# A two-block transformer in split fp32: high and low activations in one 512-column matmul

## Chip, core and metric

The kernel runs on one core of a Trainium2 chip. The metric is device time in microseconds from the first to the last instruction of the program, median of the runs; lower is better.

## What is computed

One call runs two transformer blocks over 256 positions of width 2048, all in fp32. The core of the reference:

```
x = x + hybrid_mixer(rms_norm(x), w_in, ...)          # causal pooling + gated delta net
x = x + memory_cross_attention(rms_norm(x), mem_h, w_xq, w_xkv, w_xo)
x = x + conv_glu_ffn(rms_norm(x), w_gate, w_up, ..., w_down)     # width 5632 ("FFN 1")
x = rms_norm(x, final_norm_g)
h = modulate(rms_norm_2(x, pre_norm_mix), shift_m, scale_m)
x = x + gate_m * rms_norm_2(concat(nsa_mixer(h), moba_mixer(h)) @ w_o, ...)
h = modulate(rms_norm_2(x, pre_norm_ffn), shift_f, scale_f)
x = x + gate_f * rms_norm_2(square(relu(h @ w_up)) @ w_down, ...)  # width 8192 ("FFN 2")
```

Nearly all arithmetic is in products of the 256 activations with large weights.

## The kernel before

**Split products.** A product keeps fp32 accuracy by splitting both factors into a high part (rounded to TensorE's fp32r type) and a low part (the rest). Of the four partial products three are computed: high times high, high weight times low activation, low weight times high activation. ACT writes the high weights (`wh`, L216), DVE subtracts to get the low ones (`wl`, L218).

**Units.** Weights come in groups of 512 columns of a weight matrix over all contraction blocks of 128 rows (`kb`). A unit is 1024 columns per partition, 512 KB: two contraction blocks of 512 columns. The class `Group` lists them, and `plan` fixes the order of all 880 for the whole program. `take` (called as each unit is reached) puts the split of the unit two ahead and the load of the unit up to seven ahead into the instruction streams; there are four buffers for loaded units and three for split ones.

**The two linear forms.** `lin_a` keeps activations stationary and streams 512 weight columns (L300 to L302). `lin_b` (L304) keeps 128x128 weight blocks stationary and streams the 256 activations, so that its output is transposed: features on partitions. For each contraction block and each of the four column blocks it issues three 256-column matmuls (L318 high·high, L319 high weight·low activation, L320 low weight·high activation) into the same half of a PSUM bank:

```
mm(ps, wb, h, ...); mm(ps, wb, lo, ...); mm(ps, wb2, h, ...)
```

A group of `lin_b` fills two of four accumulator banks (`acc`). 62 groups go this way: eight of `w_in`, four keys, four queries, 22 of gate and up in FFN 1, eight of the second mixer, 16 of FFN 2's up.

**Evacuation.** What follows a product is a Python generator: each `yield` ends a step, and `pump` (after every unit) lets each running task emit one step. `group_start` lets at most one older evacuation be unfinished: an older one is made to emit all that is left, at once. Engines execute their streams in order, so this fixes where each step stands. `rr_evac` multiplies each accumulator by the row of rms factors (`rr`), `conv_evac` and `gate_evac` go on with a convolution and a silu, `pool_evac` with running sums on POOL and one small matmul per window (L845), `up_evac`, `relu_evac` and `rope_evac` with their functions. `conv_evac` waits for `rr`, which a task `stats` makes from the loaded x at the start of the program (squares on ACT L378, sum on DVE L348, power on POOL L341, then two matmuls, L361). `ada` is a long background task on DVE (L1200).

**Activations.** `act_pair` holds them in four tiles: two with the high parts of 16 contraction blocks, two with the low parts.

Of the kernel before, what the change touches and what calls it, by code (L numbers as in the profile page):

```python
# [15 lines left out]
P = 128  # L16
# [73 lines left out]

class Prog:
# [3 lines left out]
    def __init__(self, ctx, tc, i, o, dbg=None):  # L95
# [16 lines left out]
        self.rr = None  # L112

# [192 lines left out]
    def lin_b(self, g, xh, xl, evac, ready=None):  # L306
        mm = self.nc.tensor.matmul
        accs = self.group_start()
        for _, kb0, nk in g.units:
            self.check_ready(ready, kb0)  # L310
            wh, wl = self.take(g)
            for k in range(nk):
                kb = kb0 + k
                h, lo = xh(kb), xl(kb)
                for b in range(4):
                    ps = accs[b // 2][:, (b % 2) * T:(b % 2 + 1) * T]
                    wb, wb2 = wh[:, k, b * P:(b + 1) * P], wl[:, k, b * P:(b + 1) * P]
                    mm(ps, wb, h, start=kb == 0 and b % 2 == 0, stop=False, skip_group_check=True)  # L318
                    mm(ps, wb, lo, start=False, stop=False, skip_group_check=True)  # L319
                    mm(ps, wb2, h, start=False, stop=kb == g.nkb - 1, skip_group_check=True)  # L320
            self.pump()
        return self.finish_group(evac([a.rearrange("p (b t) -> p b t", b=2) for a in accs]))
# [93 lines left out]
    def act_pair(self, half):  # L416

        a = [self.t(f"A{4 * half + j}", [P, 8, T], F32R) for j in range(4)]

        def part(o):  # L420
            return lambda kb, n=0: a[o + kb // 8][:, kb % 8:kb % 8 + n] if n else a[o + kb // 8][:, kb % 8, :]

        return part(0), part(2)
# [77 lines left out]
    def run(self):  # L501
# [4 lines left out]
        for n, a in (("k0", 2048), ("q0", 1024), ("v0", 3072), ("z0", 4096), ("u0", 0), ("u1", 512), ("k1", 2560),  # L506
                     ("q1", 1536), ("v1", 3584), ("z1", 4608)):
            g_in[n] = G(w_in, [(a, a + 512)])
# [4 lines left out]
        mk, mv = cols(i["w_xkv"], 4), cols(i["w_xkv"], 4, D)  # L513
        mix = [cols(i["w_mix_out"], 4, 0, 1024 * s, 8) for s in range(2)]
        xq = cols(i["w_xq"], 4)
        xo = [cols(i["w_xo"], 4, 0, 1024 * s, 8) for s in range(2)]
        self.gate, self.up = cols(i["w_gate"], 11), cols(i["w_up"], 11)
# [6 lines left out]
        b2["nq"] = cols(w2, 2)  # L524
        b2["nk1"] = G(w2, [(1024, 1536)])
        b2["nk2"] = G(w2, [(1536, 1792), (2048, 2304)])
        b2["nv"] = G(w2, [(1792, 2048), (2304, 2560)])
        b2["mq"], b2["mk"], b2["mv"] = cols(w2, 2, 2584), cols(w2, 2, 3608), cols(w2, 2, 4632)
        b2["wo"] = [cols(i["w_o_2"], 4, 0, 1024 * s, 8) for s in range(2)]
        b2["wo"][1][3:] = [G(i["w_o_2"], [(a, a + 256)], 1024, 8) for a in (1536, 1792)]  # L530
        self.up2 = cols(i["w_up_2"], 16)
# [87 lines left out]
        for name in ("silu_c", "gl16"):  # L619
            self.col(name, KB)  # L620
# [3 lines left out]
        conv0 = [self.lin_b(g_in["k0"], xh, xl, lambda a: self.conv_evac(a, S[0]["k"], "k0", 0),  # L624
                            ready={4 * c: lt[c] for c in range(4)})]
        conv0.append(self.lin_b(g_in["q0"], xh, xl, lambda a: self.conv_evac(a, S[0]["q"], "q0", 0)))
        self.start(self.ba_task(xh, xl))
        conv0.append(self.lin_b(g_in["v0"], xh, xl, lambda a: self.conv_evac(a, S[0]["v"], "v0", 0)))
# [4 lines left out]
        pools = [self.lin_b(g_in["u0"], xh, xl, lambda a: self.pool_evac(a, 0))]  # L633
        pools.append(self.lin_b(g_in["u1"], xh, xl, lambda a: self.pool_evac(a, 1)))
        conv1 = []
        for n, tag in (("k1", "r4"), ("q1", "r5"), ("v1", "r6")):
            S[1][n[0]] = self.t(tag, [P, 4, T])
            conv1.append(self.lin_b(g_in[n], xh, xl, lambda a, n=n: self.conv_evac(a, S[1][n[0]], n, 4)))
# [21 lines left out]
        def key_evac(a, c):  # L660
            yield from self.wait_for(ypt)
            kT[c] = self.t(["r8", "r9", "r7", "r11"][c], [P, 4, T])
            yield from self.rr_evac(a, kT[c], self.rrm)

        for c in range(4):
            self.lin_b(mk[c], mh, ml, lambda a, c=c: key_evac(a, c),
                       ready={4 * q: mt[q] for q in range(4)} if c == 0 else None)
# [36 lines left out]
        for c in range(4):  # L704
            qT.append(self.t(["r5", "r6", "r3", "r10"][c], [P, 4, T]))
            ev = self.lin_b(xq[c], xh, xl, lambda a, c=c: self.rr_evac(a, qT[c], self.rr))
# [30 lines left out]
    def rr_evac(self, accs, dst, row):  # L737
        for h in range(2):
            self.nc.vector.tensor_tensor(dst[:, 2 * h:2 * h + 2], accs[h], row[:, None, :].to_broadcast([P, 2, T]),
                                         op=OP.mult)  # L740
            yield
# [12 lines left out]
    def conv_evac(self, accs, dst, n, h0):  # L754
        nc = self.nc
        yield from self.until(lambda: self.rr is not None)
        st = self.t("A7" if n[0] == "q" else "A6", [P, 4, T])
        for h in range(2):
            nc.vector.tensor_tensor(st[:, 2 * h:2 * h + 2], accs[h], self.rr[:, None, :].to_broadcast([P, 2, T]),
                                    op=OP.mult)  # L760
            yield
        blk0 = {"q": 0, "k": 8, "v": 16}[n[0]] + h0
        cw = self.par("dn_conv_w")
        for b in range(4):
# [7 lines left out]
        nc.scalar.activation(dst, dst, AF.Silu)  # L772
# [42 lines left out]
    def pool_evac(self, accs, c):  # L815
        nc = self.nc
        u = self.t("r7", [P, 4, T])
        if c == 0:
# [5 lines left out]
        yield from self.rr_evac(accs, u, self.rr)  # L824
        buf = self.t("r11", [P, 2, 2, T])
        for j in range(2):
            wi = 2 * c + j
            ub = u[:, 2 * j:2 * j + 2]
            cur = ub
            for lv in range(wi + 1):  # L830
                d = 1 << lv
                nxt = buf[:, lv % 2]
                nc.gpsimd.tensor_tensor(nxt[:, :, d:], cur[:, :, d:], cur[:, :, :T - d], op=OP.add)
                nc.scalar.activation(nxt[:, :, :d], cur[:, :, :d], AF.Copy)
                cur = nxt
            yield
            mx = buf[:, wi % 2]
            nc.vector.tensor_tensor(mx, mx, self.inv[:, wi][:, None, :].to_broadcast([P, 2, T]), op=OP.mult)
            nc.vector.tensor_tensor(mx, mx, ub, op=OP.subtract)
            yield  # L840
            tag, ps = yield from self.get_bank()
            psv = ps.rearrange("p (b t) -> p b t", b=2)
            for hb in range(2):
                for gb in range(2):
                    nc.tensor.matmul(psv[:, hb], self.wpl[:, wi, gb, hb * P:(hb + 1) * P], mx[:, gb],  # L845
                                     start=gb == 0, stop=gb == 1)
            yield
            for hb in range(2):
                kb = 2 * wi + hb
                nc.scalar.activation(self.yp[c][:, 2 * j + hb], psv[:, hb], AF.Copy, scale=self.pcol("pool_scale")(kb))  # L850
            self.give(tag)
# [383 lines left out]
    def gate_evac(self, accs, c):  # L1235
        nc = self.nc
        st = self.t(f"r{c % 2}", [P, 4, T])
        cv = self.t(f"r{2 + c % 2}", [P, 4, T])
        self.cv[c] = cv
        rr = self.rr[:, None, :].to_broadcast([P, 2, T])  # L1240
        for h in range(2):
# [753 lines left out]
```

## Time and profile before

| | |
|---|---|
| median of 3 runs | 2728.45 us (2722.99 to 2728.89) |
| the profiled execution's own time | 2727.51 us |
| its span | 2725.7 us |
| TensorE busy | 2681.1 us, 98% of the span |
| DVE / ACT / POOL busy | 68% / 48% / 9% |
| DMA | 584 MB, 214 GB/s on average |

Matmuls overlap in the pipeline, so the duration of one (283 ns) is not what it costs; the distance from one start to the next is. A timeline shows it directly: the difference of two starts divided by the number of matmuls between them. "Idle before" in the groups says how long an engine stood still, and for whom.

### The profile page before, as it was taken

What the parts mean: (1) busy time and instruction counts of PE and PEld (TensorE: products, weight loads), DVE (VectorE), ACT (ScalarE), POOL (GpSimd) and SP (SyncE); (2) the same over time, 40 slices, a digit from 0 to 9 for tenths busy, and PEclk for the clock granted to TensorE, in tenths of its full rate; (3) what the DMA queues carried; (4) which work ended last, traced back from release to release, by engine and by line L of the source; (5) the groups of instructions that cost most, each with busy time, mean ns of one, the idle gap of its engine ahead of it and who ended that gap; (6) DMA issues with size and microseconds to landing.
All of it is one profiled execution on the core that took longest, in us unless ns stands there. A gap on an engine that the chain in (4) does not pass through costs nothing.

```text
span 2725.7 us, 45971 instructions
## 1 busy us (share of the span) xinstructions
PE 2681.1 (98%) x18466; PEld 2480.4 (91%) x18466; DVE 1854.2 (68%) x2331; ACT 1302.8 (48%) x1924; POOL 255.5 (9%) x229
## 2 busy tenths in 40 slices
PE   8999999999999999999999999999989999999998
PEld 8999998889989999999999888997889988999897
DVE  6665745677687778787778586677675556655555
ACT  6544533554445455354544564444554444444443
POOL 0230211000000021010100001001011000000020
PEclk9999999999999999999999999999999999999999
DMA  8644644688788888888887656544557767766654
GB/s 290 201 126 130 191 121 140 216 295 272 228 270 266 272 259 272 275 265 283 271 270 263 210 164 178 147 146 128 173 181 235 236 218 241 232 190 193 189 186 151
DMA packets 293126, 584.33 MB, mean 214 GB/s; under 512 B 21920, under 2 KB 36384, under 8 KB 292912
## 3 DMA queue, kind: packets, MB, share of 16 engines
q1 hardware_dynamic: 288528, 568.41, 65.6%
q0 software_dynamic: 3664, 11.67, 1.4%
q8 instruction: 145, 2.38, 0.4%
q10 hardware_dynamic: 720, 1.31, 0.1%
q14 instruction: 69, 0.57, 0.1%
HBM read 579.21 MB, written 2.10 MB: 213 GB/s over the span
## 4 chain that ended last, share of the span: by engine, by line
PE 93%; DVE 3%; ACT 2%; issue 1%; POOL 0%; DMA 0%; SPq 0%; DVEq 0%; POOLq 0%; ACTq 0%
PE acc L318 16%; PE acc L319 16%; PE acc L320 16%; PE acc L300 12%; PE acc L301 12%; PE acc L302 12%; DVE wl L218 1%; ACT wh L216 1%; PE m L998 1%; PE m L1051 1%; PE m L1058 1%; PE m L1148 1%; PE m L1117 1%; PE m L1001 0%; PE m L1179 0%
## 5 line engine op out<-in xcount | busy, mean ns | idle before, releaser
L218 DVE TENSOR_TENSOR wl<-w,wh 128x1024 fp32r<-128x1024 f32 x880 | 1097.1, 1249 | 805.2 <-ACT wh L216 802.8
L216 ACT ACTIVATE wh<-w 128x1024 fp32r<-128x1024 f32 x880 | 927.9, 1058 | 1121.4 <-PE acc L319 614.3
L318 PE MATMUL acc<-A,wh 128*128 128x256 f32 x3968 | 1124.1, 283 | 9.3 <-ACT A L406 7.8
L319 PE MATMUL acc<-A,wh 128*128 128x256 f32 x3968 | 1112.6, 280 | 0.7 <-DVE A L1430 0.7
L320 PE MATMUL acc<-A,wl 128*128 128x256 f32 x3968 | 1112.0, 280 | 0.8 <-DVE wl L218 0.8
L318 PEld LDWEIGHTS acc<-A,wh 128*128 128x128 f32 x3968 | 750.6, 189 | 11.4 <-ACT A L406 7.8
L320 PEld LDWEIGHTS acc<-A,wl 128*128 128x128 f32 x3968 | 756.7, 191 | 1.0 <-DVE wl L218 1.0
L319 PEld LDWEIGHTS acc<-A,wh 128*128 128x128 f32 x3968 | 749.2, 189 | 2.6 <-DVE A L1430 1.2
L300 PE MATMUL acc<-wh,A 128*128 128x512 f32 (+1 forms) x1584 | 616.0, 389 | 0.3 <-DVE r L1264 0.3
L301 PE MATMUL acc<-wl,A 128*128 128x512 f32 (+1 forms) x1584 | 608.3, 384 | 1.2 <-DVE wl L218 1.2
L302 PE MATMUL acc<-wh,A 128*128 128x512 f32 (+1 forms) x1584 | 607.8, 384 | 0.0
L301 PEld LDWEIGHTS acc<-wl,A 128*128 128x128 f32 x1584 | 298.1, 188 | 60.5 <-DVE wl L218 4.5
L302 PEld LDWEIGHTS acc<-wh,A 128*128 128x128 f32 x1584 | 297.8, 188 | 59.3
L300 PEld LDWEIGHTS acc<-wh,A 128*128 128x128 f32 x1584 | 298.0, 188 | 57.2 <-issue 0.9
L1200 DVE SCALAR_TENSOR_TENSOR r<-r,c_silu_c,r 128x1024 f32<-128x1024 f32 x128 | 170.1, 1329 | 0.0
L1200 DVE SCALAR_TENSOR_TENSOR s<-s,c_silu_c,s 128x512 f32<-128x512 f32 x128 | 95.8, 748 | 15.7 <-DMA s<-w_ada 14.4
L1886 POOL TENSOR_TENSOR s<-s 128x512 f32<-128x512 f32 x32 | 50.9, 1592 | 581.5 <-ACT s L1885 581.5
L1255 POOL TENSOR_TENSOR r<-r,rr 128x1024 f32<-128x1024 f32 x11 | 27.9, 2536 | 570.3 <-ACT r L1254 527.5
L1730 ACT ACTIVATE s<-s,c_am 128x128 f32<-128x128 f32 (+1 forms) x48 | 21.5, 448 | 92.0 <-DVE c_am L1728 92.0
L1618 POOL TENSOR_TENSOR r<-r,s 128x512 f32<-128x512 f32 x15 | 25.6, 1704 | 263.7 <-DVE s L1615 263.7
L1251 DVE SCALAR_TENSOR_TENSOR r<-r,prm,r 128x254 f32<-128x254 f32 x88 | 42.4, 481 | 1.6
L378 ACT ACTIVATE dd<-X 128x512 bf16<-128x512 f32 (+1 forms) x42 | 25.5, 606 | 21.4 <-DVE X L441 15.6
(375 smaller groups left out, 1611.8 us busy)
## 6 DMA issues: line engine op xcount, KB each, us to landing
w<-w_up SPq DMA_DIRECT2D x216, 512.0 KB, 3.8
w<-w_down SPq DMA_DIRECT2D x216, 512.0 KB, 3.9
w<-w_in SPq DMA_DIRECT2D x152, 512.0 KB, 3.7
r<-w_ada SPq DMA_DIRECT2D x128, 512.0 KB, 5.2
w<-w_gate SPq DMA_DIRECT2D x88, 512.0 KB, 4.3
w<-w_xkv SPq DMA_DIRECT2D x64, 512.0 KB, 3.9
s<-w_ada SPq DMA_DIRECT2D x128, 256.0 KB, 5.1
w<-w_mix_out SPq DMA_DIRECT2D x32, 512.0 KB, 3.7
```

The costliest lines, as they stand in the source:

```text
L216: nc.scalar.activation(hi[:, :m], src[:, :m], AF.Copy)
L218: eng.tensor_tensor(lo[:, :m], src[:, :m], hi[:, :m].bitcast(F32), op=OP.subtract)
L300: mm(ps, h, wh[:, k, :], start=kb == 0, stop=False)
L301: mm(ps, h, wl[:, k, :], start=False, stop=False)
L302: mm(ps, lo, wh[:, k, :], start=False, stop=kb == g.nkb - 1)
L318: mm(ps, wb, h, start=kb == 0 and b % 2 == 0, stop=False, skip_group_check=True)
L319: mm(ps, wb, lo, start=False, stop=False, skip_group_check=True)
L320: mm(ps, wb2, h, start=False, stop=kb == g.nkb - 1, skip_group_check=True)
L1200: nc.vector.scalar_tensor_tensor(acc, tiles.pop(n), self.silu_c[:, kb:kb + 1], acc, op0=OP.mult, op1=OP.add)
L1251: nc.vector.scalar_tensor_tensor(cv[:, b, s:], st[:, b, :T - s], w[k], cv[:, b, s:], op0=OP.mult, op1=OP.add)
L1255: nc.gpsimd.tensor_tensor(cv, cv, self.rr[:, None, :].to_broadcast([P, 4, T]), op=OP.mult)
L1886: nc.gpsimd.tensor_tensor(y, y, y, op=OP.mult)
```

## The change

The high and low activations of one contraction block now lie next to each other, so that one matmul with a high weight block streams both, 512 columns; the low weight block adds its 256 into the second half. One PSUM bank then holds high·high in its first half and the two cross products in the second, and the evacuation adds the halves first (`fold`): ACT copies the second half out, DVE adds the first. A 512-wide group becomes a `Pair` of two 256-wide ones, each of four units of four contraction blocks (same bytes, rows of 1 KB instead of 2 KB), each with its two banks and its own evacuation. The first pairs of six stages (`widen`) run unit by unit side by side in all four banks.

```
+class Pair:
+    def __init__(self, w, a, b=None):
+        self.subs = [Group(w, [(c, c + 256)]) for c in (a, b)]
+        self.units = self.subs[0].units + self.subs[1].units
+    def widen(self):
+        self.units = [u for two in zip(*(g.units for g in self.subs)) for u in two]
...
+    def lin_b(self, pair, xh, xl, evac, ready=None):
+        if pair.wide:
+            while self.evacs:
+                self.need(self.evacs.pop(0))
+            accs = [[self.acc(), self.acc()] for _ in range(2)]
...
+    def unit_b(self, g, n, accs, xh, ready):
...
+            for b in range(2):
+                mm(accs[b], wb, xh.both(kb).rearrange("p j t -> p (j t)"), start=kb == 0, ...)
+                mm(accs[b][:, T:], wb2, xh(kb), start=False, stop=kb == g.nkb - 1, ...)
+    def fold(self, accs, dst):
+        for b in range(2):
+            self.nc.scalar.activation(dst[:, b], accs[b][:, 1], AF.Copy)
+            self.nc.vector.tensor_tensor(dst[:, b], accs[b][:, 0], dst[:, b], op=OP.add)
...
-        a = [self.t(f"A{4 * half + j}", [P, 8, T], F32R) for j in range(4)]
+        a = [self.t(f"A{4 * half + j}", [P, 4, 2, T], F32R) for j in range(4)]
...
+        for p in (g_in["k0"], mk[0], xq[0], self.gate[0], b2["nk1"], self.up2[0]):
+            p.widen()
...
     def rr_evac(self, accs, dst, row):
-        for h in range(2):
-            self.nc.vector.tensor_tensor(dst[:, 2 * h:2 * h + 2], accs[h], row[...], op=OP.mult)
+        self.fold(accs, dst)
+        yield
+        self.nc.vector.tensor_tensor(dst, dst, row[...], op=OP.mult)
...
     def pool_evac(self, accs, j, c):
...
         nc.vector.tensor_tensor(mx, mx, ub, op=OP.subtract)
+        for _ in range(3):
+            yield
         tag, ps = yield from self.get_bank()
```

The other evacuations change alike: fold, a step, then what they did before, on half the columns per task.

**First place: TensorE, from the program's first group (`k0`) to its second (`q0`).** Rows are line, operation, out<-in, shape. Before, the two matmuls that make `rr` (from `dd`) stand inside `q0`, after the first matmuls of its third unit:

```order
L320 MATMUL acc_23_421<-A_5_98,wl_424 128x256
L318 MATMUL acc_24_422<-A_5_98,wh_423 128x256
L319 MATMUL acc_24_422<-A_7_100,wh_423 128x256
L320 MATMUL acc_24_422<-A_5_98,wl_424 128x256
L318 MATMUL acc_24_422<-A_5_98,wh_423 128x256
L319 MATMUL acc_24_422<-A_7_100,wh_423 128x256
L320 MATMUL acc_24_422<-A_5_98,wl_424 128x256
L361 MATMUL m_26_521<-dd_488,cst 128x128 x2
```

Now they stand right ahead of `q0`'s first matmul:

```order
L355 MATMUL acc_14_120<-A_8_101,wl_279 128x256
L353 MATMUL acc_13_119<-A_8_101,wh_278 128x512
L355 MATMUL acc_13_119<-A_8_101,wl_279 128x256
L353 MATMUL acc_14_120<-A_8_101,wh_278 128x512
L355 MATMUL acc_14_120<-A_8_101,wl_279 128x256
L401 MATMUL m_27_374<-dd_371,cst 128x128 x2
L353 MATMUL acc_30_391<-A_5_98,wh_308 128x512
L355 MATMUL acc_30_391<-A_5_98,wl_309 128x256
L353 MATMUL acc_31_392<-A_5_98,wh_308 128x512
L355 MATMUL acc_31_392<-A_5_98,wl_309 128x256
```

Each triple of 256-column matmuls has become a 512-column and a 256-column one, and the `rr` matmuls have moved three units forward.

**The same place on DVE.** Before, the weight splits (`wl`) go on, and the first group's evacuation (L759) begins between the splits of later units:

```order
L218 TENSOR_TENSOR wl_354<-w_8_203,wh_353 128x1024
L218 TENSOR_TENSOR wl_388<-w_9_238,wh_387 128x1024
L218 TENSOR_TENSOR wl_424<-w_10_273,wh_423 128x1024
L348 TENSOR_REDUCE c_mix_r_s<-c_mix_p 128x2
L218 TENSOR_TENSOR wl_459<-w_11_319,wh_458 128x1024
L357 TENSOR_SCALAR dd_488<-cst,c_mix_r 128x128
L218 TENSOR_TENSOR wl_492<-w_12_357,wh_491 128x1024
L759 TENSOR_TENSOR A_29_528<-acc_11_116,rr_524 128x512
L218 TENSOR_TENSOR wl_531<-w_13_391,wh_530 128x1024
L759 TENSOR_TENSOR A_29_528<-acc_12_117,rr_524 128x512
```

Now the fold (L362) and the whole evacuation of the first half of `k0` stand between the splits of units 9 and 10 (`w_9_...` and `w_10_...`):

```order
L234 TENSOR_TENSOR wl_335<-w_9_217,wh_334 128x1024
L362 TENSOR_TENSOR A_25_360<-acc_11_117,A_25_360 128x256
L362 TENSOR_TENSOR A_25_360<-acc_12_118,A_25_360 128x256
L388 TENSOR_REDUCE c_mix_r_s<-c_mix_p 128x2
L397 TENSOR_SCALAR dd_371<-cst,c_mix_r 128x128
L813 TENSOR_TENSOR A_25_360<-A_25_360,rr_377 128x512
L821 SCALAR_TENSOR_TENSOR A_9_112<-A_25_360,prm,A_9_112 128x253
L821 SCALAR_TENSOR_TENSOR A_9_112<-A_25_360,prm,A_9_112 128x254
L821 SCALAR_TENSOR_TENSOR A_9_112<-A_25_360,prm,A_9_112 128x255
L821 SCALAR_TENSOR_TENSOR A_9_112<-A_25_360,prm,A_9_112 128x253
L821 SCALAR_TENSOR_TENSOR A_9_112<-A_25_360,prm,A_9_112 128x254
L821 SCALAR_TENSOR_TENSOR A_9_112<-A_25_360,prm,A_9_112 128x255
L234 TENSOR_TENSOR wl_394<-w_10_244,wh_393 128x1024
```

Eleven instructions now stand between two weight splits that followed each other before.

**Second place: DVE in FFN 1, a gate group's evacuation.** Before (L1200 is `ada`, L1251 the convolution):

```order
L218 TENSOR_TENSOR wl_11888<-w_354_11763,wh_11887 128x1024
L1200 SCALAR_TENSOR_TENSOR r_718_11310<-r_747_11727,c_silu_c,r_718_11310 128x1024
L1242 TENSOR_TENSOR r_753_11920<-acc_744_11629,rr_8575 128x512
L218 TENSOR_TENSOR wl_11924<-w_355_11796,wh_11923 128x1024
L1242 TENSOR_TENSOR r_753_11920<-acc_745_11630,rr_8575 128x512
L218 TENSOR_TENSOR wl_11955<-w_356_11826,wh_11954 128x1024
L1200 SCALAR_TENSOR_TENSOR r_718_11310<-r_748_11790,c_silu_c,r_718_11310 128x1024
L1251 SCALAR_TENSOR_TENSOR r_754_11921<-r_753_11920,prm,r_754_11921 128x254
L1251 SCALAR_TENSOR_TENSOR r_754_11921<-r_753_11920,prm,r_754_11921 128x255
L218 TENSOR_TENSOR wl_11991<-w_357_11859,wh_11990 128x1024
```

Now:

```order
L234 TENSOR_TENSOR wl_9572<-w_318_9471,wh_9571 128x1024
L362 TENSOR_TENSOR r_764_9593<-acc_757_9465,r_764_9593 128x256
L362 TENSOR_TENSOR r_764_9593<-acc_758_9466,r_764_9593 128x256
L234 TENSOR_TENSOR wl_9600<-w_319_9501,wh_9599 128x1024
L1255 SCALAR_TENSOR_TENSOR r_717_8940<-r_756_9439,c_silu_c,r_717_8940 128x1024
L1301 TENSOR_TENSOR r_764_9593<-r_764_9593,rr_7648 128x512
L1309 SCALAR_TENSOR_TENSOR r_765_9594<-r_764_9593,prm,r_765_9594 128x254
L1309 SCALAR_TENSOR_TENSOR r_765_9594<-r_764_9593,prm,r_765_9594 128x255
L234 TENSOR_TENSOR wl_9629<-w_320_9524,wh_9628 128x1024
L1309 SCALAR_TENSOR_TENSOR r_765_9594<-r_764_9593,prm,r_765_9594 128x254
L1309 SCALAR_TENSOR_TENSOR r_765_9594<-r_764_9593,prm,r_765_9594 128x255
L234 TENSOR_TENSOR wl_9654<-w_321_9548,wh_9653 128x1024
```

Two more instructions per half group have come (L362), and the multiplication by `rr` (L1301) shares its step with the first convolution block.

## Rows read from the trace of the kernel before

**Rows 1.** The page, parts 1 and 2: engines over the span; TensorE clock by slice.

```profile
PE 2681.1 (98%) x18466; PEld 2480.4 (91%) x18466; DVE 1854.2 (68%) x2331; ACT 1302.8 (48%) x1924; POOL 255.5 (9%) x229
...
PEclk9999999999999999999999999999999999999999
```

**Rows 2.** The page, part 4: the chain that ended last, by engine.

```profile
PE 93%; DVE 3%; ACT 2%; issue 1%; POOL 0%; DMA 0%; SPq 0%; DVEq 0%; POOLq 0%; ACTq 0%
```

**Rows 3.** Groups by line and shape, TensorE: xcount, busy us, mean ns, idle before.

```profile
L318 PE MATMUL acc<-A,wh 128*128 128x256 f32 x3968 | 1124.1, 283 | 9.3 <-ACT A L406 7.8 <-ACT A L1425 1.5
...
L300 PE MATMUL acc<-wh,A 128*128 128x512 f32 x1488 | 588.7, 396 | 0.3 <-DVE r L1264 0.3
```

**Rows 4.** TensorE timeline, FFN 1, start us, us: two starts, 48 matmuls apart.

```profile
1000.03 0.28 PE L320 MATMUL acc<-A,wl 128*128 128x256 f32 x1
...
1005.68 0.28 PE L320 MATMUL acc<-A,wl 128*128 128x256 f32 x1
```

**Rows 5.** The same, later in FFN 1: two starts, 24 matmuls apart.

```profile
1310.04 0.28 PE L318 MATMUL acc<-A,wh 128*128 128x256 f32 x1
...
1312.76 0.28 PE L318 MATMUL acc<-A,wh 128*128 128x256 f32 x1
```

**Rows 6.** The same, during the delta-net stage: two starts, 22 matmuls apart.

```profile
307.39 0.28 PE L319 MATMUL acc<-A,wh 128*128 128x256 f32 x1
...
310.03 0.28 PE L320 MATMUL acc<-A,wl 128*128 128x256 f32 x1
```

**Rows 7.** The same, a 512-column group: two starts, 12 matmuls apart.

```profile
2469.94 0.39 PE L300 MATMUL acc<-wh,A 128*128 128x512 f32 x1
...
2472.66 0.39 PE L300 MATMUL acc<-wh,A 128*128 128x512 f32 x1
```

**Rows 8.** Timelines of ACT, DVE, POOL and TensorE at the start of the program.

```profile
31.60 0.19 ACT L378 ACTIVATION_READ_ACCUMULATOR dd<-X 128x1 f32 x1
...
57.23 1.28 ACT L772 ACT_TABLE_LOAD   x1 [2.75 <-DVE A L769]
...
34.03 0.15 DVE L348 TENSOR_REDUCE c_mix_r_s<-c_mix_p 128x2 f32<-128x8 f32 x1
...
34.56 0.70 POOL L341 TENSOR_TENSOR c_mix_r<-c_mix_r,mhalf 128x2 f32<-128x2 f32 x1
...
40.55 0.49 PE L361 MATMUL m<-dd,cst 128*128 128x128 f32 x2 [0.75 <-ACT dd L356]
41.72 0.49 PE L361 MATMUL m<-dd,cst 128*128 128x128 f32 x2 [0.68 <-DVE dd L357]
```

**Rows 9.** Groups by line and shape, DVE, then ACT.

```profile
L218 DVE TENSOR_TENSOR wl<-w,wh 128x1024 fp32r<-128x1024 f32 x880 | 1097.1, 1249 | 805.2 <-ACT wh L216 802.8
L1200 DVE SCALAR_TENSOR_TENSOR r<-r,c_silu_c,r 128x1024 f32<-128x1024 f32 x128 | 170.1, 1329 | 0.0
...
L1251 DVE SCALAR_TENSOR_TENSOR r<-r,prm,r 128x254 f32<-128x254 f32 x44 | 21.1, 478 | 0.0
...
L1242 DVE TENSOR_TENSOR r<-acc,rr 128x512 f32<-128x512 f32 x22 | 15.1, 684 | 0.0
...
L1578 DVE TENSOR_TENSOR r<-acc,r 128x256 f32<-128x256 f32 x8 | 3.0, 421 | 3.0 <-PE acc L302 3.0
...
L363 ACT ACTIVATE rr<-m 128x256 f32<-128x256 f32 x5 | 1.9, 384 | 5.9 <-PE m L361 5.8
```

**Rows 10.** Groups by line: the two DVE steps before a pool matmul.

```profile
L839 DVE TENSOR_TENSOR r<-r,r 128x512 f32<-128x512 f32 x4 | 3.5, 872 | 0.1
...
L838 DVE TENSOR_TENSOR r<-r,A 128x512 f32<-128x512 f32 x4 | 3.0, 744 | 0.0
```

**Rows 11.** Busy by engine in the stretch of two gate and two up groups.

```profile
core 0: us, PE busy (x) PEld busy (x) DVE busy (x) ACT busy (x) POOL busy (x), PEclk, DMA share, GB/s
1121.00:1211.00 90.00, 90.00 (x772) 89.92 (x771) 68.66 (x72) 43.77 (x60) 5.49 (x4) 1.00 0.81 265
```

**Rows 12.** DMA issues in two stretches: 256-wide groups, then 512-wide; us to landing.

```profile
w<-w_down SPq DMA_DIRECT2D x6, 512.0 KB, 3.7
...
w<-w_up SPq DMA_DIRECT2D x14, 512.0 KB, 3.8
```

More of the change, by code (lines that the diff above doesn't have):

```diff
@@ L112, in __init__ @@
         self.rr = None
+        self.stage = {}
     def t(self, tag, shape, dt=F32):
@@ L304, in lin_a @@
         return self.finish_group(evac(accs), eager)
-    def lin_b(self, g, xh, xl, evac, ready=None):
-        mm = self.nc.tensor.matmul
[L308 to L322, printed above, removed]
+    def lin_b(self, pair, xh, xl, evac, ready=None):
+        task = None
+        if pair.wide:
+            while self.evacs:
+                self.need(self.evacs.pop(0))
+            accs = [[self.acc(), self.acc()] for _ in range(2)]
+            for n in range(len(pair.subs[0].units)):
+                for g, a in zip(pair.subs, accs):
+                    self.unit_b(g, n, a, xh, ready)
+        for j, g in enumerate(pair.subs):
+            if not pair.wide:
+                a = self.group_start()
+                for n in range(len(g.units)):
+                    self.unit_b(g, n, a, xh, ready)
+            else:
+                a = accs[j]
+            gen = evac([x.rearrange("p (j t) -> p j t", j=2) for x in a], j)
+            task = self.finish_group(self.chain(self.wait_for(task), gen) if task else gen)
+        return task
@@ new lines, in unit_b @@
+    def unit_b(self, g, n, accs, xh, ready):
+        mm = self.nc.tensor.matmul
+        _, kb0, nk = g.units[n]
+        self.check_ready(ready, kb0)
+        wh, wl = self.take(g)
+        for k in range(nk):
+            kb = kb0 + k
+            for b in range(2):
+                wb, wb2 = wh[:, k, b * P:(b + 1) * P], wl[:, k, b * P:(b + 1) * P]
+                mm(accs[b], wb, xh.both(kb).rearrange("p j t -> p (j t)"), start=kb == 0, stop=False,
+                   skip_group_check=True)
+                mm(accs[b][:, T:], wb2, xh(kb), start=False, stop=kb == g.nkb - 1, skip_group_check=True)
+        self.pump()
@@ L618, in run @@
         A5 = self.t("A5", [P, 2, 4, T])
-        for name in ("silu_c", "gl16"):
+        for name in ("silu_c", "gl16", "beta"):
             self.col(name, KB)
@@ L771, in conv_evac @@
             yield
-        nc.scalar.activation(dst, dst, AF.Silu)
+        d2 = dst[:, 2 * j:2 * j + 2]
+        nc.scalar.activation(d2, d2, AF.Silu)
         yield
@@ L823, in pool_evac @@
             nc.gpsimd.dma_start(self.wpl, self.i["w_pool"][0].rearrange("n (b p) h -> p n b h", p=P))
[L824 to L835, printed above, removed]
-            yield
[L837 to L851, printed above, removed]
@@ new lines, in pool_evac @@
+        if j == 0:
+            self.stage["u"] = self.t("r7", [P, 4, T])
+            self.stage["b"] = self.t("r11", [P, 2, 2, T])
+        buf = self.stage["b"]
+        ub = self.stage["u"][:, 2 * j:2 * j + 2]
+        yield from self.rr_evac(accs, ub, self.rr)
+        wi = 2 * c + j
+        cur = ub
+        for lv in range(wi + 1):
+            d = 1 << lv
+            nxt = buf[:, lv % 2]
+            nc.gpsimd.tensor_tensor(nxt[:, :, d:], cur[:, :, d:], cur[:, :, :T - d], op=OP.add)
+            nc.scalar.activation(nxt[:, :, :d], cur[:, :, :d], AF.Copy)
+            cur = nxt
@@ new lines, in pool_evac @@
+        yield
+        mx = buf[:, wi % 2]
+        nc.vector.tensor_tensor(mx, mx, self.inv[:, wi][:, None, :].to_broadcast([P, 2, T]), op=OP.mult)
+        nc.vector.tensor_tensor(mx, mx, ub, op=OP.subtract)
+        for _ in range(3):
+            yield
+        tag, ps = yield from self.get_bank()
+        psv = ps.rearrange("p (b t) -> p b t", b=2)
+        for hb in range(2):
+            for gb in range(2):
+                nc.tensor.matmul(psv[:, hb], self.wpl[:, wi, gb, hb * P:(hb + 1) * P], mx[:, gb],
+                                 start=gb == 0, stop=gb == 1)
@@ L852, in pool_evac @@
+        yield
+        for hb in range(2):
+            kb = 2 * wi + hb
+            nc.scalar.activation(self.yp[c][:, 2 * j + hb], psv[:, hb], AF.Copy, scale=self.pcol("pool_scale")(kb))
+        self.give(tag)
         yield
```

187 lines of the change are left out of this document (99 added, 88 removed).

## Prediction

> **What bounds the kernel now.** I read the engines' shares first. TensorE is busy for 2681.1 of 2725.7 us, and its clock is at the top of the scale in all forty slices, so no time is to be had from the clock; DVE is busy for 68% and ACT for 48% [rows 1]. The chain of waits says the same from behind: 93% of what ended last lies on TensorE, 3% on DVE [rows 2]. So TensorE's own stream sets the time. The groups by line give the stream's make-up: 3968 products of one weight block with 256 activations, each as three matmuls, and 512-column matmuls in the other form [rows 3]. A matmul's duration there (283 ns) overlaps its neighbours', so I went to timelines and divided distances between starts.
>
> They show three speeds for the 256-column form: 48 matmuls in 5.65 us, 117.7 ns each [rows 4]; 24 in 2.72 us, 113.3 ns [rows 5]; 22 in 2.64 us, 120.0 ns [rows 6]. A speed holds for long stretches and then changes. Counted over 495 undisturbed units of 24 matmuls, 155 run at 113.3, 316 near 117.7 and 24 near 120. The 512-column form, outside the delta-net stage, has one speed: 12 in 2.72 us, 226.7 ns [rows 7]. That is twice 113.3, so a column costs the same in both, and the 4.4 and 6.7 ns on top belong to the matmul, not to its columns.
>
> **The change, part by part. Streaming.** A unit's eight triples become eight pairs of one 512 and one 256. No row of before has the two forms in turn, so the pair is bounded:
> - At best the long matmul covers whatever delays the next, and a pair costs 226.7 + 113.3 = 340.0 ns in every stretch. The triple costs 340.0, 353.1 or 360.0. Saved per unit: 0, 8 × 13.1 = 105 ns, 8 × 20 = 160 ns. Sum: 316 × 0.105 + 24 × 0.160 = 37 us.
> - At worst the 512 pays the 6.7 ns [rows 6] too and the 256 runs at 120.0 everywhere: 353.4 ns. The 155 fast units lose 8 × 13.4 = 107 ns (16.6 us), the 316 neither lose nor gain, the 24 gain 8 × 6.6 ns (1.3 us): a loss of 15 us.
> - I take the nearest rows for each half: the 512 at 226.7, as everywhere that it is alone, and the 256 at the speed of its stretch. Pairs of 340.0, 344.4 and 346.7 save 0, 8.7 and 13.3 ns: 316 × 8 × 8.7 = 22 us and 24 × 8 × 13.3 = 2.6 us, together **25 us**.
>
> **New waits.** (a) *The first two groups.* `q0` needs two free banks at its first unit and so forces the first half of `k0` out, three units sooner than before, which is 3 × 2.72 = 8.2 us [rows 5]. In front of it stands the chain that makes `rr`: last square at 31.79 us, sum at 34.03, power on POOL 0.70 us, two matmuls at 40.55 and 41.72 which already wait 0.75 and 0.68 us; then a Silu that loads its table for 1.28 us [rows 8]. On DVE eleven instructions come ahead of the split of unit 10: six convolution steps of about 0.48, a product of 0.68, two adds of 0.42 [rows 9], 4.4 us in all with the small ones left out, plus 1.25 for the split; units 8 and 9, already split, cover 5.4. So the split is just in time, and the `rr` matmuls are not. Between 2 us (the chain closes at its bare durations) and 8 us (the whole advance is waiting) I take +5.
>
> (b) *The four pool matmuls.* `group_start` of the next group forces them out straight behind the two DVE steps that they read, 0.74 + 0.87 = 1.6 us [rows 10]; the three empty steps put in between are cut short by the same forcing. TensorE meets the wait with nothing queued in between: 0 if other tasks' matmuls cover it, one unit each (10.9 us) if POOL's sums are late too. I take 4 × 1 = +4.
>
> (c) *Heads of the five other wide stages.* A fold of both banks takes 384 + 384 + 421 ns at least and 1.6 us one after another [rows 9]; the next group takes the banks. The wide order has two evacuations fall due at once where before there was one; a unit is 2.7 us. Between 0 and 1.6 each, I take 0.6 each: +3.
>
> Together +12, between 2 and 27.
>
> **What I cost at nothing.** The other half groups' folds: the banks of the half before last are taken over four units after it ended, 10.9 us, so a fold of 1.6 us is hidden; without that cover it would cost 1.6 × 112, which is a rival below. Two adds per half group: in a stretch of two gate and two up groups DVE is busy for 68.66 of 90.0 us and ACT for 43.77 [rows 11]; 16 adds of 0.421 make 75.4, 16 copies of 0.384 make 49.9, against some 88 us: 86% and 57%. The heaviest unit there has a split (1.25), an `ada` step (1.33), a product (0.68) and two convolution steps (0.96), 4.2 us against 2.75, which the split-ahead of two units absorbs. Loads of 1 KB rows: 256-wide blocks land in 3.7 us, 512-wide ones in 3.8 [rows 12], with up to seven units of lead. The activations' new tiles are split at the same contraction blocks and are waited for at the same places.
>
> **Sum.** 2727.5 (the profiled execution's own time) − 25 + 12 = 2714.5. The median of the runs stands 0.9 us above that execution, so 2715.
>
> **The rivals.** *R1, a larger gain.* If what delays a 256-column matmul is something that 226.7 ns of streaming hides, half of the boundaries lose it and the other half run ahead of it. For it: no 512-column stretch without other work shows the 4.4 ns. Against it: the pair still holds a 256, behind which the next high weight must come. 37 us off, waits near 5 to 10: 2695 to 2701.
>
> *R2, columns alone count.* 226.7 is exactly two times 113.3; the three speeds belong to stretches, not to places in the triple, and what makes them is not in the profile. If a stretch keeps its extra per column, the pair costs what the triple cost and only waits remain: 2728 + 2 to 12 = 2730 to 2740. The Trainium skill ("TensorE: Matmul & The Clock Gate", section Back-to-back issue gap) gives a warm matmul N/2.4 + 2.5 ns, so one issue fewer would be worth 2.5 ns a triple whatever the stretch, an estimate of 10 us, and with my waits the time would end at about 2730; the rows here, 113.3 and 226.7 ns, are both longer than it says and show no such constant at that speed.
>
> *R3, slower: DVE becomes the bound.* Its queue is in order, and every added add waits for its ACT copy (0.38 us), which the busy count leaves out. Place: the gate and convolution stages, where each half group now puts two such waits ahead of the next split. DVE goes from 76% to 86% there [rows 11]; it decides from the point at which busy time and waits pass the 88 us, which takes 0.8 us of wait for each of the 16 adds, twice a copy. Then splits come late and TensorE waits for `wl`. At 0.4 us per half group and 124 half groups this is 50 us: 2728 − 25 + 12 + 50 = 2765. Against it: DVE stands idle 805 us ahead of splits now, nearly all of it for ACT's high weights [rows 9].
>
> That the change does something else than it says is excluded by the order of its instructions: 3968 matmuls of each width in the new form, the same units in the same stages.
>
> **How the numbers follow.** The forecast (2703 to 2724) has 0.42, R1 0.24, R2 0.19, R3 0.11, and 0.04 is for what I do not see. The range runs from 2692 (R1 with few waits) to 2742 (R2 with all of its waits); R3 and the unseen lie outside. A measurement can tell about 0.2% from no change, 5.5 us, so between 2723 and 2734. Faster: the forecast but for its edge, and R1: 0.64. Same: that edge and half of R2: 0.14. Slower: the rest of R2, R3 and half of the unseen: 0.22.
>
> **What would show it right or wrong.** Timelines of FFN 1 and FFN 2 should show pairs of 344 ns, and 340 where the stretch is fast; 340 everywhere is R1, 353 where the triple took 353 is R2. At the start, TensorE should wait a few microseconds for `rr` at `q0`'s first matmul, and 1 to 2 us at each pool matmul. In FFN 1 DVE's share should be near 86% with no wait of TensorE for `wl`; waits there are R3. Landing times of loads should stay under 4 us. Wrong in its reasons would be a gain that comes from fewer waits, or a loss in a place not named here.

## The result and the profile after

| | before | after the change |
|---|---|---|
| median of the runs | 2726.68 us (4 runs) | 2775.72 us (4 runs) |
| ratio | | 1.018, 95% interval 1.0168 to 1.0191 |
| span of the profiled execution | 2725.7 us | 2773.6 us |

Predicted were 2715 us and a range up to 2742. The change made the kernel 49 us slower.

The page of the profile after, parts 1, 2 and 4, lines that answer to [rows 1, 2]:

```profile
PE 2704.8 (98%) x14498; PEld 2315.0 (83%) x14498; DVE 1936.7 (70%) x2579; ACT 1370.3 (49%) x2187; POOL 253.0 (9%) x240
...
PEclk9999999999999999999999999999999999999999
...
PE 88%; DVE 4%; ACT 3%; issue 2%; POOL 1%; DMA 1%; SPq 0%; DVEq 0%; POOLq 0%; ACTq 0%
```

TensorE issues 3968 matmuls fewer, as meant, and is busy 24 us longer. It is still the engine that ends last, but its share of the chain went from 93 to 88%, and DVE, ACT, POOL, DMA and issue have one point more each: new waits. DVE's busy share rose by two points only.

Where the time came from is read by walking both timelines side by side, from one linear form's stage to the next (start of the stage's first matmul, us):

| stage that ends here | before | after | gap so far |
|---|---|---|---|
| first twelve units (`k0`, half of `q0`) | 44.8 | 51.8 | 7.0 |
| first mixer with the delta net, keys | 419.7 | 436.4 | 16.7 |
| mixer's output, values | 612.9 | 629.8 | 16.9 |
| queries | 721.6 | 742.9 | 21.3 |
| attention's output, FFN 1's first six groups | 963.0 | 990.7 | 27.7 |
| FFN 1, the rest | 1476.5 | 1509.5 | 33.0 |
| last of FFN 1, second mixer's first four groups | 1681.4 | 1724.4 | 43.0 |
| second mixer's rest | 1997.4 | 2042.6 | 45.2 |
| FFN 2 and the end | 2725.7 | 2773.6 | 47.9 |

Two things stand in it. Where a stage is nothing but streaming, the change gains nothing: five of FFN 2's seven up stages take 45.2 us in both kernels, and the steady stages of FFN 1 become up to 3 us longer. And most of the other rows lose 2 to 10 us each.

**The stream.** TensorE's timeline of the kernel after, FFN 1 (start, duration), two starts 30 matmuls apart:

```profile
1020.24 0.40 PE L353 MATMUL acc<-A,wh 128*128 128x512 f32 x1
1020.48 0.28 PE L355 MATMUL acc<-A,wl 128*128 128x256 f32 x1
1020.60 0.40 PE L353 MATMUL acc<-A,wh 128*128 128x512 f32 x1
...
1025.54 0.40 PE L353 MATMUL acc<-A,wh 128*128 128x512 f32 x1
```

Fifteen pairs take 5.30 us, 353.3 ns each: the 512 takes 235 where the other linear form's takes 226.7 [rows 7], the 256 takes 118. Of 3,829 pairs that follow each other directly 3,261 take 353 or 354 ns, one takes 340; 300 lie between 343 and 349, about half of them beside the delta net (300 to 436 us). 353.3 is three times 117.7 [rows 4]: the pair costs what the slow triple cost, and more than the fast one [rows 5].

**The waits.** What TensorE waited for in the kernel after (us in total, times, longest):

```profile
PE m L401 <- ACT dd L396: 5.6, 2, 3.1
PE acc L353 <- DVE r L362: 4.9, 3, 2.2
PE m L900 <- DVE r L893: 4.9, 3, 2.4
...
PE acc L353 <- DVE A L1488: 3.4, 2, 2.3
PE acc L355 <- DVE wl L234: 3.4, 7, 0.8
```

L401 stands for the `rr` matmuls, L362 the fold, L900 the pool matmuls; L1488 writes split activations. The long waits have a tail. TensorE's timeline at the head of `q0` and the granted clock behind it:

```profile
36.60 0.71 PE L401 MATMUL m<-dd,cst 128*128 128x128 f32 x4 [2.50 <-ACT dd L396]
...
37.63 0.63 PE L353 MATMUL acc<-A,wh 128*128 128x512 f32 x1
38.06 0.41 PE L355 MATMUL acc<-A,wl 128*128 128x256 f32 x1
38.27 0.63 PE L353 MATMUL acc<-A,wh 128*128 128x512 f32 x1
```

```profile
core 0: us, PE busy (x) PEld busy (x) DVE busy (x) ACT busy (x) POOL busy (x), PEclk, DMA share, GB/s
37.10:40.60 3.50, 3.50 (x13) 2.96 (x13) 2.19 (x5) 1.29 (x3) 0.00 (x0) 0.53 1.07 374
40.60:44.00 3.40, 3.40 (x21) 2.97 (x20) 1.32 (x3) 1.92 (x3) 0.00 (x0) 0.98 0.80 275
```

After standing for 2.50 us the engine runs its next pairs at up to 640 ns instead of 353; the clock of that stretch is 0.53, near the lower level (1.2 GHz), and 0.98 in the next. Six pairs take 3.74 us instead of 2.12, 1.6 us more. The same happens behind the fold waits at 652 and 871 us (2.2 us each, clock 0.51 and 0.50) and behind the other waits of 2.2 us and more in this trace, the program's first apart, for which it holds no clock. It is not so in every run: in the run with a looser forcing below, a fold wait of 2.47 us at 872 us has the clock at 1.00 behind it.

```profile
874.60 0.47 PE L372 MATMUL acc<-A,wh 128*128 128x512 f32 x1 [2.47 <-DVE r L381]
```

```profile
875.00:878.50 3.50, 3.50 (x22) 3.05 (x21) 2.36 (x5) 1.42 (x3) 0.00 (x0) 1.00 0.51 181
```

The kernel before had such tails too: [rows 1] shows a clock of 9 tenths and more in all forty slices, but a slice is 68 us long, and between the program's start and end the trace has the lower level for 20.5 us. After the change it is 37.6 us.

### The profile page after: what moved, and what is told of

Its sections match the earlier page's. It is cut to its first block, busy times and chain, and to the rows that moved or that the text cites. A ratio compares the mean times of both kernels' runs of the same rounds, so it can differ in the third digit from the quotient of the medians.

```text
span 2773.6 us, 38568 instructions
## 1 busy us (share of the span) xinstructions
PE 2704.8 (98%) x14498; PEld 2315.0 (83%) x14498; DVE 1936.7 (70%) x2579; ACT 1370.3 (49%) x2187; POOL 253.0 (9%) x240
## 4 chain that ended last, share of the span: by engine, by line
PE 88%; DVE 4%; ACT 3%; issue 2%; POOL 1%; DMA 1%; SPq 0%; DVEq 0%; POOLq 0%; ACTq 0%
PE acc L353 30%; PE acc L355 15%; PE acc L316 12%; PE acc L317 12%; PE acc L318 12%; DVE wl L234 2%; ACT wh L232 1%; PE m L1053 1%; PE m L1106 1%; PE m L1113 1%; DMA s<-w_ada 1%; PE m L1172 0%; PE m L1203 0%; PE m L1056 0%; ACT dd L418 0%
## 5 line engine op out<-in xcount | busy, mean ns | idle before, releaser
L353 PE MATMUL acc<-A,wh 128*128 128x512 f32 x3968 | 1431.7, 403 | 19.5 <-DVE A L447 8.8
L353 PEld LDWEIGHTS acc<-A,wh 128*128 128x128 f32 x3968 | 752.5, 190 | 201.5 <-DVE A L447 9.1
L1313 POOL TENSOR_TENSOR r<-r,rr 128x512 f32<-128x512 f32 x22 | 33.1, 1506 | 562.8 <-ACT r L1312 562.8
L1306 ACT ACTIVATE r<-r,prm 128x256 f32<-128x256 f32 x44 | 26.0, 594 | 61.3 <-DVE r L1301 61.3
L362 DVE TENSOR_TENSOR r<-acc,r 128x256 f32<-128x256 f32 x116 | 43.4, 415 | 6.9 <-ACT r L361 6.9
L362 DVE TENSOR_TENSOR s<-acc,s 128x256 f32<-128x256 f32 x108 | 40.4, 416 | 0.0
```

Source lines behind the costliest of these rows:

```text
L353: mm(accs[b], wb, xh.both(kb).rearrange("p j t -> p (j t)"), start=kb == 0, stop=False, skip_group_check=True)
L362: self.nc.vector.tensor_tensor(dst[:, b], accs[b][:, 0], dst[:, b], op=OP.add)
L1313: nc.gpsimd.tensor_tensor(c2, c2, rr, op=OP.mult)
```

## The experiments

Times are medians; the kernel before took 2726.6 to 2728.1 us beside them, the change 2775.7.

**Triples again, all else as after the change.**

```
-mm(accs[b], wb, xh.both(kb)...)
+mm(accs[b][:, :T], wb, xh(kb), ...)
+mm(accs[b][:, T:], wb, xh.both(kb)[:, 1], ...)
 mm(accs[b][:, T:], wb2, xh(kb), ...)
```

> Every pair is written as three 256-column matmuls again (high.high into the first half of the bank, the two cross products into the second); groups, wide stages, folds and waits stay as they are after the change. Theory A (the pair holds a slow speed: 353 ns in 3,600 of 3,829 pairs, while the triple of before ran a part of its stretches at 340): the stretches that follow a pause come back to 113.3 ns a matmul, 8 to 17 us off, 2759 to 2768. Theory B (the speed belongs to the stretch and is paid by the column, whatever the form): 2775 within 4 us. Theory C (my prediction: the form alone saves): slower than the change by up to 25 us, 2800.

2761.56 us, ratio to before 1.0134 (1.0117 to 1.0151): 14 us better than the change, as Theory A had it; Theories B and C are out. So the 512-column form costs about 14 us in the same structure, and everything else that the change brought (half groups, folds, wide heads) about 34. Of these, waits between this form's own matmuls are 14 (22.6 us in this run against 8.1 before), and the places where other matmuls come in between are 18 longer. What a matmul takes above 113.3 ns per 256 columns, summed over the steps of this form that no wait, slow clock or other matmul lengthens, is 37 us before, 48 after the change and 31 here. This sum is called the excess below.

**No wide heads.**

```
-for p in (g_in["k0"], mk[0], xq[0], self.gate[0], b2["nk1"], self.up2[0]): p.widen()
```

> None of the six stages starts with its pairs side by side; the rest is the change. Theory W (the wide heads turn two evacuations into one wait and the wait into a slow clock: 2.2 us twice on folds, with some 1.5 to 2 us of slow pairs behind each, and 2.5 us for rr at the start): 6 to 12 us off, 2764 to 2770, and no wait on the fold at the heads of keys and queries. Rival (any first group waits for the same fold, since its banks are the ones that come free): no change within 4 us, and the waits sit one group later.

2778.51 us, 1.0198 (1.0178 to 1.0218). The fold waits are gone, and others stand in their place; the first of TensorE's waits in this kernel:

```profile
PE acc L353 <- DVE A L1486: 13.3, 8, 2.4
PE acc L353 <- DVE A L447: 9.8, 3, 7.9
```

L1486 and L447 write the split activations (7.9 us of L447 are the program's start, as in every run). A half group alone runs through all contraction blocks in four units instead of eight, so at the head of a stage it asks for its activations in half the time. The second mixer's first stage and FFN 2's first became 12 and 7 us longer than before (10 and none in the change), queries and FFN 1's head 4 and 3 shorter than in the change. The theory fell: wide heads only choose which wait is taken.

**Seven orders of the same work in FFN 2.**

```
+for c, form in enumerate(("pair", "unit", "triple", "lowfirst", "block", "alone", "tunit", "pair")): ...
```

> The sixteen up groups of FFN 2 take seven orders, two groups each, all behind the same 512-column stage: pair; all 512s of a unit, then its 256s; triple; 256 ahead of 512; 512s of a contraction block, then its 256s; 512s alone (groups 10 and 11 leave low weights times high activations out); eight 256s of each kind in turn; pair. Theory A (mixing two widths holds the slow speed): runs of 512s at 226.7 ns, as in the other linear form, and 235 only where widths alternate. Theory B (the speed belongs to the stretch and is paid by the column): every order 0.460 ns a column, 512s alone at 235. Theory L (each load of weights costs some 6.7 ns): 512s alone 233, triples 360 for 768 columns, pairs 353 in every order.

One run, 2758.13 us. The first up groups behind a 512-column stage, in ns for two 512s and two 256s or as many columns:

| order | one after another | sum |
|---|---|---|
| 512, 256 in turn; 256 ahead of 512 | 235, 118 | 706 |
| triples, in either order | 117.7 | 706 |
| all 512s of a unit, then its 256s | 236 and 231 in turn; 118, then 113 | 693 |
| two 512s, two 256s | 226, 236, 118, 113 | 693 |
| 512s alone | 236 and 231 in turn | |

TensorE's timeline of the two-and-two order (x2: two like it in a row):

```profile
2357.85 0.63 PE L356 MATMUL acc<-A,wh 128*128 128x512 f32 x2
2358.32 0.40 PE L359 MATMUL acc<-A,wl 128*128 128x256 f32 x2
2358.55 0.62 PE L356 MATMUL acc<-A,wh 128*128 128x512 f32 x2
2359.02 0.39 PE L359 MATMUL acc<-A,wl 128*128 128x256 f32 x2
```

Blocks start 0.70 us apart. None of the three theories holds as it was put. The order matters, against B; 512s alone are not at 226.7, against A; weight loads alone don't set it, against L, which had 360 for the triple and 353 for every order. The sums fall on few values: per 768 columns 340, 346.7, 353.3, and 360 with [rows 6], in steps of 6.7 ns.

**The new form in the feed-forward layers alone.**

```
+self.lin_p(self.gate[c], ...)   # gate, up of FFN 1, up of FFN 2: pairs
 self.lin_b(g_in["k0"], ...)     # all other groups as before the change
```

> Only gate and up of FFN 1 and up of FFN 2 (38 of 62 groups) take the new form; the first mixer, keys, queries and the second mixer are as before the change. Theory P (the loss is the waits of the irregular stages, about +45 of the 48 us, and the steady stages gain nothing): the steady stages are 0 to 3 us longer each where before ran at 113 ns, 7 us in all, so 2731 to 2738. Rival (the new evacuation costs TensorE everywhere, spread thin): in proportion to the groups, 38/62 of 48 us, 2757. Rival (my prediction's streaming gain shows once the waits are gone): 2710.

2740.86 us, 1.0053 (1.0036 to 1.0069). The first mixer, queries and second mixer come back to before's times within about 1 us. The 14 us left lie where they were forecast and at one more place: FFN 1's steady stages 6 us (0, 0.8, 2.0 and 3.1, more the more of the stage had run at 113.3), FFN 2 some 2, and 5 at FFN 1's wide head, which keeps its fold wait (1.8 us). Theory P was right in the steady stages (7 us forecast, 8 found); the wide head was not in it.

**Two 512s, then two 256s, everywhere.**

```
+for b in range(2):
+    mm(accs[b], wh[...], both, ...)
+for b in range(2):
+    mm(accs[b][:, T:], wl[...], xh(kb), ...)
```

> As the change, but in each contraction block the two 512-column matmuls come first, then the two 256-column ones (in the run with seven orders: 226, 236, 118, 113 ns, 693 a block, where two pairs took 706). Theory O (the order of widths sets the speed): 62 groups x 32 blocks x 2 halves = 3,968 / 2 blocks by 13 ns = 26 us off, 2750, a little less where the delta-net stage already had 347 a pair. Theory S (the speed belongs to the stretch, and that stretch had a better one by chance): 2775 within 5 us.

2754.38 us, 1.0103 (1.0088 to 1.0118): 21 us off by an order of instructions alone, all of it streaming (the excess falls from 48 to 27 us), so Theory O stands; the first mixer's eight groups still take 20 us longer than before. The run is still 28 us slower than the kernel before.

**Seven more orders.**

```
+for c, form in enumerate(("pair", "cross", "two", "bmajor", "rev", "swap", "mirror", "tblock")): ...
```

> Seven more orders in FFN 2's up groups, two groups each (W is a 512, v a 256, with the column block's number): pair; W0 W1 v0 W0 v1 W1 crossed over; two contraction blocks at a time, WWWW vvvv; four W then four v of one column block; v0 v1 W0 W1; W1 W0 v1 v0; W0 W1 v1 v0; triples with their three kinds in turn, two by two. Theory O: the time of a matmul goes by the width of the one behind it, 236 where a 256 follows a 512 and 118 where a 256 follows a 256 first, so that fewer changes of width cost less: two blocks at a time 686 to 693 per four matmuls, crossed 706. Theory S: all at one speed within a stage. If the column block's address matters, the swapped orders show other numbers than 226, 236, 118, 113.

One run, 2768.38 us. Every order with two or more of a width in a row took 693 ns for two 512s and two 256s (16 units 44.2 to 44.3 us from first to last matmul, 45.2 in the one stage that other matmuls interrupt); crossed over and in turn 706; triples two by two 706. Swapping the column blocks changed no number, so the address is not it. No order of the two widths reached 680.

**Pushing the triple.** In the kernel before, an extra matmul into a bank that is about to be cleared anyway:

```
+for w in getattr(g, "nudge", ()):
+    mm(accs[0][:, :w], wh[:, 0, :P], two[:, :w], start=True, stop=True, ...)
```

> The kernel before, with one to four extra matmuls ahead of the first triple of seven of FFN 2's up stages, whose results are thrown away (512; 512 twice; 128; 128 four times; 512 and 128; 384; 512 four times). Before, a stage that follows the 512-column form ran at 117.7 ns from its first to its last matmul. Theory K (the speed is a phase that is set at the entry and kept): some of the seven run all their 16 units at 113.3, 1.7 us a stage less the extra matmul; others at 117.7 or 120. Rival (the speed comes from what else the stage does: loads, evacuation, memory traffic): all seven at 117.7.

One run, 2724.39 us. TensorE's timelines of two stages behind the same kind of stage, first with one 384-column extra (L315), then with one of 128:

```profile
2489.45 0.34 PE L315 MATMUL acc<-A,wh 128*128 128x384 f32 x1
...
2489.99 0.28 PE L322 MATMUL acc<-A,wh 128*128 128x256 f32 x1
2490.10 0.28 PE L323 MATMUL acc<-A,wh 128*128 128x256 f32 x1
2490.22 0.28 PE L324 MATMUL acc<-A,wl 128*128 128x256 f32 x1
2490.33 0.28 PE L322 MATMUL acc<-A,wh 128*128 128x256 f32 x1
```

```profile
2222.81 0.22 PE L315 MATMUL acc<-A,wh 128*128 128x128 f32 x1
...
2223.27 0.28 PE L322 MATMUL acc<-A,wh 128*128 128x256 f32 x1
2223.39 0.28 PE L323 MATMUL acc<-A,wh 128*128 128x256 f32 x1
2223.51 0.28 PE L324 MATMUL acc<-A,wl 128*128 128x256 f32 x1
2223.62 0.28 PE L322 MATMUL acc<-A,wh 128*128 128x256 f32 x1
```

From its second triple on the first stage runs at 113.3 ns (0.34 us a triple), to its end: 43.5 us instead of 45.2. The second stays at 117.7 to its end. One extra of 384 or 512, two or four of 512 gave the fast speed; one or four of 128, and 512 with 128 behind it, did not. (The stage with 512 and 128 went from 117.7 to 113.3 later, behind other matmuls that come in between after two units; the same stage of the kernel before does so at the same place.) Up to that break, and in the other stages to their end, the kernel before runs at 117.7 with the same loads and evacuations, so Theory K is shown for triples: the speed is decided at the entry and kept until something comes between. Each kind of entry stands in one stage of one run here; that of 384 was repeated below.

**The push where it pays: 15 groups of the kernel before.**

```
+some = [gate[0], up[0]] + [gate[c] for c in (1, 3, 5, 7, 9)] + up2[1:2] + up2[2::2]
+if kb0 == 0 and id(g) in self.nudged:
+    mm(accs[0][:, :384], wh[:, 0, :P], two[:, :384], start=True, stop=True, ...)
```

> The kernel before, with one thrown-away 384-column matmul at the head of 15 groups: the first gate and up, the first gate of the five later stages of FFN 1, the second up group of FFN 2 and the first of its seven later pairs. In the run with seven kinds of extra matmul that one turned a stage of 16 units from 117.7 to 113.3 ns a matmul, for 0.2 us. Theory K (a phase, set at the entry and kept): stages that ran at 117.7 run at 113.3: FFN 2 six by 1.5 us and 2.8 for the first stretch, FFN 1 about 3 + 3.2 + 2.3 + 1.3 + 0.4 us; 15 to 20 us in all, 2707 to 2712, 0.6 to 0.7% faster than before. Rival (the entry decides by chance, each stage anew): a part of it, 2715 to 2727.

**2705.64 us, ratio 0.9927 (0.9915 to 0.9940)**: faster than both kernels. One of FFN 2's stages, its extra matmul, and the first matmul of the next stage (L300):

```profile
2119.41 0.34 PE L314 MATMUL acc<-A,wh 128*128 128x384 f32 x1
2119.58 0.28 PE L321 MATMUL acc<-A,wh 128*128 128x256 f32 x1
...
2163.12 0.39 PE L300 MATMUL acc<-wh,A 128*128 128x512 f32 x1
```

384 matmuls in 43.54 us, 113.4 ns each. Five of FFN 2's stages are 1.5 us shorter, the first stretch 2.5, FFN 1's 4.6, 3.2, 2.4, 1.2 and 0.1: the term that was forecast, 21 us where 15 to 20 were. The excess fell from 37 to 14.5 us; less the 15 extra matmuls, that is nearly the whole gain.

**The push at all 62 groups.**

```
+some = every group of this linear form
```

> The same extra matmul at the head of all 62 groups of the kernel before. Theory K: more stages at 113.3 (keys, queries and the mixers too: 10 + 12 units by 0.1 us and some), against 47 more extra matmuls of 0.2 us, 9 us: within 5 us of the run with 15 of them, on either side. Rival (a second push throws a fast stretch back): above 2715.

2711.56 us, 0.9951 (0.9937 to 0.9964), 6 us above the run with 15. The excess is 14.0 us, hardly lower: the gain forecast for keys, queries and mixers did not come, and the 47 extra matmuls cost 8 us more of plain streaming. A push is worth its 0.2 us where many units follow undisturbed.

**A half group forced only up to its fold, in the first mixer.**

```
-    self.need(self.evacs.pop(0))
+    self.need_banks(self.evacs.pop(0))
...
+task = task or (self.last_loose if loose else None)
 task = self.finish_group(self.chain(self.wait_for(task), gen) if task else gen)
```

> The change, but in the first mixer's eight groups a new group forces the older half group only up to its fold, which is what sets the banks free; the multiplication by rr, the convolutions and the pool steps follow one step a unit. Theory F (the forcing puts the rr chain and the pool matmuls ahead of their inputs: 2.5 us and slow pairs at the head of q0, 2.4 us four times or less at the pool matmuls): the 5 us at units 7 to 9 and 5 to 8 us around the pools go, 2763 to 2768. Rival (those inputs are late by themselves, the waits only move): 2772 to 2779.

2776.15 us, 1.0188 (1.0173 to 1.0203): no gain. The first of TensorE's waits there:

```profile
PE acc L372 <- DVE A L381: 12.5, 5, 7.2
PE acc L372 <- DVE A L467: 8.2, 1, 8.2
...
PE acc L372 <- DVE r L381: 6.6, 5, 2.5
```

The wait for `rr` at `q0` is gone (unit 7 takes 3.5 us instead of 6.0), and four units on TensorE waits 7.2 us for the fold (L381) of the next half: a half's evacuation starts only when that of the half before has ended, and that one now has its convolutions still to do. Theory F's forecast fell and the rival's came. The edit kept this order of the halves and extended it from one group to the next; a fold let ahead of the older half's convolutions was not tried, so that four units are too short for a half group in any order is not shown.

**The push on pairs.**

```
+for c, (form, ws) in enumerate((("pair", ()), ("pair", (384,)), ("pair", (512,)), ("pair", (512, 512)),
+                                ("rev", (384,)), ("swap", (384,)), ("triple", (384,)), ("pair", (128,)))): ...
```

> The change, with extra thrown-away matmuls at the head of FFN 2's up stages: pairs with none, 384, 512, 512 twice and 128; v0 v1 W0 W1 with 384; W1 W0 v1 v0 with 384; triples with 384. Theory K for triples: 113.3 ns after 384. For pairs: if their 353 is a phase too, one of the four entries gives 340 or 347; if the change of widths makes it anew with every pair, all four stay at 353, and the change's form has no better speed to be pushed into.

One run, 2773.86 us. TensorE's timeline behind the entry of 384:

```profile
2091.88 0.34 PE L372 MATMUL acc<-A,wh 128*128 128x384 f32 x1
2092.05 0.39 PE L356 MATMUL acc<-A,wh 128*128 128x512 f32 x1
2092.28 0.28 PE L359 MATMUL acc<-A,wl 128*128 128x256 f32 x1
2092.40 0.39 PE L356 MATMUL acc<-A,wh 128*128 128x512 f32 x1
```

The first three pairs take 344 to 347 ns, and then they are at 353 again for the rest. Behind all four entries pairs settled at 235 and 118 within four pairs, two-and-two orders at their 693. Triples of the same kernel, with the same evacuation, went to 113.3: 43.4 us for the stage from first to last, where the pairs took 45.1. So the pair, unlike the triple, did not keep a better speed by these means.

## Why the prediction was wrong

**The step that failed is the streaming term.** It read 113.3, 117.7 and 120.0 ns as a column cost and an addition that would "belong to the matmul, not to its columns", and counted two of a triple's three additions as saved, 25 us. The runs show something else in its place: a speed of the stream, which lands on a few values per 768 columns and goes by the order of the widths, and in triples also by the entry, which sets it until the next break. The pair sits on the second slowest of these values, 353.3, nearly everywhere, its 512 paying in proportion. Where the triple had been slow the change gained nothing; where it had been fast, it lost. The summed excess went from 37 to 48 us instead of down by 25: 36 us off in this term alone, and 14 us is what the triples give back in the same structure.

The evidence was in [rows 4 to 6]: stretches, not places in the triple, had the speeds. R2 said so and had 0.19; it named half of the result (353 where the triple took 353) and gave a range up to 2740. That the fast stretches would be lost it did not say. The row that misled was [rows 7]: 226.7 ns in a stage whose weights and activations have other roles; it was no witness for a 512 in this one (231 to 236 alone in the third experiment). The lower bound, a loss of 15 us, was nearest: in the runs the excess grew by 11. That bound and the upper one of the waits, 27, together make 2770 us; the stated range left both out by ending at 2742, R2 with waits of 12.

Beside R2 the prediction set a rule of the Trainium skill ("TensorE: Matmul & The Clock Gate", section Back-to-back issue gap), N/2.4 + 2.5 ns a matmul, an estimate of 10 us saved. The trace disagrees: a pair takes 353.3 ns, no less than the slow triple.

**New waits** were put at 12 us, 27 at most; the runs give about 34 for the structure. (a) The head: 7.0 us at unit 12, forecast 5 in 2 to 8. The wait for `rr` came where it was said, but that the size fits is in part luck: the stretch at the `rr` matmuls costs 3.1 us where the one before cost 2.3. The slow clock behind it takes 1.6, pairs at 353 where the triples ran at 340 take 1.0, the program's first units 1.9. And the split of unit 10, which the prediction held to be just in time, was late on ACT, behind the Silu that waited for the convolutions; TensorE's two waits for it cost 1.7 in all:

```profile
44.99 0.51 PE L353 MATMUL acc<-A,wh 128*128 128x512 f32 x1 [0.50 <-ACT wh L232]
46.25 0.39 PE L355 MATMUL acc<-A,wl 128*128 128x256 f32 x1 [0.75 <-DVE wl L234]
```

(b) The pool matmuls: 4.9 us of waiting, forecast 4. (c) The wide heads: 2.2 us at queries and at FFN 1, forecast 0.6 each; two evacuations due at once, as said, but the fold ended later than its bare 1.6 us. What the sum left out was the tail (the prediction had read in [rows 1] that no time is to be had from the clock): where the clock fell behind a wait of 2.2 to 2.5 us, the slow pairs cost some 1.6 us more, so that such a wait counted nearly double. Left out too was that the delta-net and attention tasks start at other places and meet other waits: of the first mixer's 17 us 7 are the head and 5 the pool matmuls; the rest, and most of the second mixer's 10, stand in no term. In the second mixer's first four groups 166 matmuls of other tasks come in between, 133 before. No run separated these parts.

**R3** did not come: DVE's share in FFN 1's steady stages is 82 to 87%, forecast 86, and no wait for `wl` stands in them. In the whole kernel such waits rose from 2.0 to 7.1 us, 1.8 of it in FFN 1's first six groups, far from the 50 us of R3. Loads of `w_gate` landed in 4.8 us (4.3 before), those of `w_down` in 4.5 (3.9 before), those of `w_up` in 3.8 as before; so the sign of "under 4 us" did not hold even before, and no wait of TensorE is put down to a load.

## To carry to other kernels

When a stream shows several spacings that hold for long stretches, find out what sets them before pricing an instruction saved: count where they change, and push one stage with a throw-away instruction. A half-sized group halves the time in which its inputs and evacuation must be ready, and here neither a looser forcing nor another order of the halves did more than choose which wait was paid. When TensorE stands still for a few microseconds, look at the granted clock behind the wait and price the slow stretch with it.

## What the runs showed of the hardware

A stream of 256-column fp32r matmuls on this chip ran at 113.3, 117.7 or 120.0 ns a matmul in the same loop, at the first two for hundreds in a row; one 384-column matmul ahead of it turned 117.7 into 113.3 at each place in FFN 2 where it was put. Mixed widths took 346.7 or 353.3 ns per 768 columns by their order; pairs pushed in the same way were back at 353.3 within four pairs. What inside the engine makes these steps was not found.
